# A hybrid attention step: queues ordered by a four-pass planner with due times, and one more query tile turned by VectorE and a transfer

## The chip, the cores and the metric

The kernel runs on one core of a Trainium2 chip. A core has a matrix engine (TensorE, PE in the profile; its weight loads are the row PEld), three engines for elementwise work (VectorE is DVE, ScalarE is ACT, GpSimd is POOL), a sync engine (SP) that in this kernel issues every transfer, and 16 DMA engines. Each engine works through its own queue in the order in which the program lists its instructions, and waits on semaphores. The metric is the device time of one execution, in microseconds, as the median of several runs.

## The reference, cut to what matters

One layer of a streaming encoder on 1024 prompt rows and 32 sample rows of width 1024, all in float32.

```python
qa, ka, va, ga, qb, kb, vb, gb = split(rmsnorm(h, g_pre) @ w_in)      # 1024 -> 8 x 512
# A: 8 heads of 64, band attention: a frame reads its own 64-frame chunk and the 8 before it
s = q @ k.T * ATTN_SCALE + bias_table[clip(k_pos - q_pos)];  oa = softmax(where(ok, s, NEG_INF)) @ v
# B: 8 heads of 64, stick-breaking attention, strictly causal
z = q @ k.T * ATTN_SCALE
log_1m = where(causal, log_sigmoid(-z), 0);  after = reverse_cumsum(log_1m) - log_1m
ob = where(causal, exp(log_sigmoid(z) + after), 0) @ v
y = concat(oa * silu(ga), ob * silu(gb)) @ w_out
h = h + rmsnorm(y, g_post)
h = h + sigmoid(h @ w_ple_gate) * (p @ w_ple)
```

The keys and values are returned too.

## The kernel before, in words

**Stages.** The rows are normalised, transposed and split into a high and a low half of fp32r (`hnh`, `hnl`), so that three fp32r matmuls make one float32 product. Then the 32 column blocks of `w_in` are multiplied (tiles `mm_qA`, `mm_kB`, ..., each in three chunks of 352 rows, 24 matmuls a chunk), woven with the attention of 16 heads, A and B in turn. The gates (`mm_gA`, `mm_gB`) come last and run beside the last head. Two Strassen-like stages follow: `w_out` (tiles `o0P` to `o3P`) and `w_ple_gate` (`g0P` to `g3P`).

**One head of B.** For each of eight query tiles `i` of 128 rows, `scores(i)` makes the scores against the `i + 1` key blocks up to it in PSUM (`SB`), ScalarE takes a Sigmoid into `om`, VectorE a running product (the scan), and GpSimd the difference of neighbours into `be`: the weights, query by key. TensorE needs them key by query. `weights_t(i)` turns them and splits the result into `wTh` (ScalarE's cast) and `wTl` (VectorE's subtraction). It has two ways:

- with TensorE: 128x128 transposes in groups of four into PSUM (`ptw`), from which the halves are made;
- for tiles named in `ROUND` (the dictionary `together`): VectorE turns 32x32 squares from `be` into `om`, a transfer writes `om` to a scratch tensor (`swap`), four transfers bring its quarters back into `be` in block order, and the halves are made from `be` in SBUF.

In `ROUND` before, tiles 4 and 6 of every head go the second way, of A and of B. Then `values(g)` multiplies the turned weights of four query tiles with the values (`PVB`). `attention_stream` lists the steps: tile `i`'s turning two units after its scores, and the values behind the last tile of a group of four. The last head of B runs from tile 7 down.

`om` and `be` are places in two rings of SBUF (`Arena`, 3076 and 3328 columns); a tile's place is given away when all its uses are done. The scores of tile 5 of B are 768 columns wide, those of tile 4 640, of tile 6 896.

**The order of the queues.** The program first only records its operations (`Recorder`). `Recorder.order` then lays them out on a model of the engines: at each step it takes the engine that can start first, and on it the waiting operation with the smallest key. The key is a class and the place in the program: class 0 for attention and 1 for projections on TensorE, `low` on the other engines. `cost` gives each operation's duration and how long after it its result can be used. A transfer is counted as an issue of 600 ns, 1500 ns of latency, the time of its bytes on one shared line, and 2000 ns of margin; a result that TensorE uses counts 400 ns more. The order that comes out is the order in which `emit` issues the instructions, so it is fixed when the program is built: on the chip, each engine waits in that order.

Of the kernel before, what the change touches and what calls it, by code (L numbers as in the profile page):

```python
# [8 lines left out]
F32 = mybir.dt.float32  # L9
F32R = mybir.dt.float32r  # L10
AF = mybir.ActivationFunctionType
# [16 lines left out]

ROUND = {"A": ((4,),(6,)), "B": ((4,),(6,))}
LAG_T = 2
LAG_V = 2
SPACE_S = 0.1
# [138 lines left out]


class Op:
    __slots__ = ("eng", "what", "args", "kw", "key", "busy", "late", "ready", "left", "after", "at", "size", "shared")


LAND = {"PE": 165, "ACT": 0, "DVE": 0, "POOL": 0, "SP": 0, "CTL": 0}
SEM = 60  # L180
MARGIN = 400
ISSUE = 600
DMA_NS, DMA_RATE, DMA_MARGIN = 1500, 320.0, 2000
DVE_SET, POOL_SET = 137, 110


# [77 lines left out]
class Recorder:  # L264
# [35 lines left out]
    def node(self, eng, what, args, kw, after):  # L300
        o = Op()
        o.eng, o.what, o.args, o.kw, o.after = eng, what, args, kw, after
        o.key = (self.cls if eng == "PE" else self.low, len(self.ops))
        o.shared = False
        self.ops.append(o)
        return o

    def add(self, eng, what, args, kw):
        writes, reads = [], []
        method = what[1] if isinstance(what, tuple) else ""  # L310
        for i, a in enumerate(args):
            if isinstance(a, (View, Raw, Segments)):
                (writes if i == 0 or (method == "tensor_tensor_reduce" and i == 7) else reads).append(a)
        for k, a in kw.items():
            if isinstance(a, (View, Raw, Segments)):
                (writes if k in ("out", "accum_out") else reads).append(a)
        o = self.node(eng, what, args, kw, set())
        for mine, write in ((reads, False), (writes, True)):
            for v in mine:
                b = v.buf  # L320
                hit = False
                for other, box, wrote in b.uses:
                    if other is not o and (write or wrote) and all(p < y and x < q for (p, q), (x, y) in zip(v.box, box)):
                        o.after.add(other)
                        hit = True
                if b.pool is not None:
                    if not hit:
                        o.after.add(b.place)
                    b.pool.ops.append(o)
                b.uses.append((o, v.box, write))  # L330
        o.busy, o.late = self.cost(eng, method, args, kw, writes, reads)
        o.shared = eng == "POOL"
        if eng == "DVE":
            sbuf = [v for v in reads if isinstance(v, (View, Segments)) and not v.buf.psum and v.free() > 4]
            o.shared = len(sbuf) > 1 or (method == "tensor_copy" and len(sbuf) == 1 and not writes[0].buf.psum)

    @staticmethod
    def cost(eng, method, args, kw, writes, reads):

        out = writes[0] if writes else None  # L340
        n = out.free() if isinstance(out, View) else 1
        psum = any(isinstance(v, (View, Segments)) and v.buf.psum for v in reads)
        if eng == "PE":
            if method == "transpose":
                return (109 if args[1].shape[0] > 64 else 62), 165
            return max(109.0, 2.5 + 0.449 * args[2].free()) * (1 if args[2].buf.dtype == F32R else 4), 165
        if eng == "ACT":
            return (60 if psum else 95) + 0.83 * n + (190 if "accum_out" in kw else 0), 105
        if eng == "DVE":
            if method == "tensor_tensor_scan":  # L350
                return 120 + 2.1 * n, 85
            if method == "tensor_copy" and not psum:
                return 70 + 0.53 * n, 85
            if method == "scalar_tensor_tensor":
                return 125 + 1.04 * n, 85
            if method == "tensor_tensor_reduce":
                return 90 + 1.04 * n, 150
            return 70 + 1.04 * n, 85
        if eng == "POOL":
            if method == "tensor_tensor":  # L360
                if n == 1:
                    return 535, 40
                return 170 + (1.77 if out.buf.dtype == F32 else 2.15) * n, 40
            if method == "tensor_scalar":
                return 255 + 0.86 * n, 0
            return 100 + 0.82 * n, 0
        size, run = 4, 0
        for v in (out, args[1]):
            if isinstance(v, View) and v.buf.pool is not None:
                size, run = 4 * v.shape[0] * v.free(), 4 * v.shape[-1]  # L370
        return ISSUE, max(size / DMA_RATE, size / run * (8.5 + 0.0365 * run) / 16)


    def order(self):

        import heapq
        for place, old in self.turns:
            place.after.update(x[0] for x in old.uses)
        users = {id(o): [] for o in self.ops}
        for o in self.ops:  # L380
            o.left, o.ready = len(o.after), 0.0
            for a in o.after:
                users[id(a)].append(o)
        names = ("PE", "ACT", "DVE", "POOL", "SP", "CTL")
        free = dict.fromkeys(names, 0.0)
        soon = {e: [] for e in names}
        now = {e: [] for e in names}
        for o in self.ops:
            if not o.left:
                heapq.heappush(soon[o.eng], (0.0, o.key, id(o), o))  # L390
        out, port, line = [], 0.0, 0.0
        while len(out) < len(self.ops):
            best = None
            for e in names:
                if now[e]:
                    t = free[e]
                elif soon[e]:
                    t = max(free[e], soon[e][0][0])
                else:
                    continue  # L400
                if best is None or t < best[0]:
                    best = (t, e)
            t, e = best
            while soon[e] and soon[e][0][0] <= t:
                _, key, n, o = heapq.heappop(soon[e])
                heapq.heappush(now[e], (key, n, o))
            o = heapq.heappop(now[e])[2]
            if o.shared and e == "DVE" and port > t + DVE_SET:
                held = [x for x in now[e] if not x[2].shared]
                if held:  # L410
                    heapq.heappush(now[e], (o.key, id(o), o))
                    pick = min(held)
                    now[e].remove(pick)
                    heapq.heapify(now[e])
                    o = pick[2]
            o.at = t
            if e == "CTL":
                done = t
            elif e == "SP":
                free[e] = t + o.busy  # L420
                line = max(line, t + o.busy + DMA_NS) + o.late
                done = line + DMA_MARGIN
            else:
                if o.shared:
                    t = max(t, port - (DVE_SET if e == "DVE" else POOL_SET))
                    port = t + o.busy
                free[e] = t + o.busy
                done = t + o.busy + o.late
            out.append(o)
            for u in users[id(o)]:  # L430
                if u.eng == e and e != "SP":
                    r = t if e == "CTL" else free[e] if e == "PE" else done
                else:
                    r = done + (0 if u.eng == "CTL" else SEM + (MARGIN if u.eng == "PE" else 0))
                u.ready = max(u.ready, r)
                u.left -= 1
                if not u.left:
                    heapq.heappush(soon[u.eng], (u.ready, u.key, id(u), u))
        return out


    def emit(self, tc):
# [15 lines left out]
def stream_step(  # L458
# [79 lines left out]
    def load_w(j):  # L538

        if j >= len(order) or j in raws:  # L540
            return
        kind, p = order[j]
        c0 = NAMES.index(kind) * 512 + p * P
        raws[j] = []
        for kh in range(2):
            raw = wpool.tile([P, 4, P], F32, tag="wr", name=f"wr_{kind}{p}_{kh}", bufs=4)
            dma(raw, w_in[0, kh * 512:(kh + 1) * 512, c0:c0 + P].rearrange("(k p) c -> p k c", p=P))
            raws[j].append(raw)
# [243 lines left out]
    def attention(ab, p, h):  # L792
# [16 lines left out]

        together = {i: g for g in ROUND[ab] for i in g}  # L810
        whole, done_with = {}, []
# [901 lines left out]
    for m, (nm, src, group) in enumerate(sets):  # L1713
        last_set = m == len(sets) - 1
        state = [{}, {}]
        for n, prod in enumerate(ORDER):
            for pair, t in enumerate(group):
# [43 lines left out]
                if nm == "o":  # L1761
# [4 lines left out]
                    if prod == "P6":  # L1766
                        add(up, st["p1"], bank, ALU.add)
# [101 lines left out]
```

## Time and profile before

| | before |
|---|---|
| median of 3 runs | 804.93 us (804.59 to 805.31) |
| the profiled execution | 809.23 us |
| its span, first to last instruction | 807.4 us |
| granted TensorE clock, mean | 0.998 |
| TensorE busy | 788.0 us, 98% of the span |
| VectorE, ScalarE, GpSimd busy | 70%, 62%, 54% |
| moved by the DMA engines | 161.09 MB, 199 GB/s on average |

A busy time is the time in which at least one instruction of the engine is under way. Matmuls overlap, so their mean durations add up to more than the busy time. All operations are issued from one line of the program (`emit`, L452), so the rows are told apart by the tiles they write and read (out<-in).

### The profile page before, as it was taken

What the parts mean: (1) busy time and instruction counts of PE and PEld (TensorE: products, weight loads), DVE (VectorE), ACT (ScalarE), POOL (GpSimd) and SP (SyncE); (2) the same over time, 40 slices, a digit from 0 to 9 for tenths busy, and PEclk for the clock granted to TensorE, in tenths of its full rate; (3) what the DMA queues carried; (4) which work ended last, traced back from release to release, by engine and by line L of the source; (5) the groups of instructions that cost most, each with busy time, mean ns of one, the idle gap of its engine ahead of it and who ended that gap; (6) DMA issues with size and microseconds to landing.
All of it is one profiled execution on the core that took longest, in us unless ns stands there. A gap on an engine that the chain in (4) does not pass through costs nothing.

```text
span 807.4 us, 14271 instructions
## 1 busy us (share of the span) xinstructions
PE 788.0 (98%) x4646; PEld 722.3 (89%) x4646; DVE 567.9 (70%) x1007; ACT 504.4 (62%) x1061; POOL 432.1 (54%) x503
## 2 busy tenths in 40 slices
PE   8999989999999999999999999999999999999997
PEld 7899989899989999899999989999997777878786
DVE  7626768786588788788886688765435787477655
ACT  5636774676586646795675696543327977877641
POOL 5623655764356668134551236777542549598513
PEclk9999999999999999999999999999999999999999
DMA  8419895667878749854535667765569948869633
GB/s 276 149 45 293 215 253 175 195 185 217 225 225 246 215 121 267 216 146 133 151 81 169 147 175 212 234 199 152 166 207 322 298 147 270 278 218 302 215 108 131
DMA packets 160973, 161.09 MB, mean 199 GB/s; under 512 B 39154, under 2 KB 120794, under 8 KB 160899
## 3 DMA queue, kind: packets, MB, share of 16 engines
q1 hardware_dynamic: 160898, 160.18, 67.1%
q8 instruction: 37, 0.61, 0.3%
q14 instruction: 38, 0.30, 0.1%
HBM read 99.23 MB, written 52.49 MB: 188 GB/s over the span
## 4 chain that ended last, share of the span: by engine, by line
PE 72%; DMA 6%; ACT 6%; POOL 5%; DVE 5%; issue 4%; SPq 2%; DVEq 0%; POOLq 0%; ACTq 0%
PE mm_gA L452 6%; PE mm_gB L452 6%; PE mm_kA L452 5%; PE mm_qA L452 5%; PE mm_qB L452 4%; PE SB L452 3%; PE mm_vA L452 3%; PE PVB L452 3%; PE mm_kB L452 3%; PE PVA L452 3%; PE mm_vB L452 3%; PE SA L452 2%; PE o1P L452 2%; PE g2P L452 2%; PE g3P L452 2%
## 5 line engine op out<-in xcount | busy, mean ns | idle before, releaser
L452 POOL TENSOR_TENSOR be<-om 128x128 f32<-128x128 f32 (+7 forms) x64 | 75.4, 1184 | 64.8 <-DVE om L452 29.0
L452 DVE TENSOR_TENSOR_SCAN om<-om,SB 128x384 f32<-128x384 f32 (+5 forms) x96 | 94.9, 1001 | 9.1 <-ACT om L452 7.4
L452 ACT ACTIVATE om<-SB 128x384 f32<-128x384 f32 (+5 forms) x96 | 44.4, 493 | 36.0 <-DVE SB L452 26.9
L452 ACT ACTIVATE be<-om,statA 128x640 f32<-128x640 f32 (+3 forms) x64 | 44.4, 694 | 18.2 <-DVE statA L452 11.0
L452 DVE TENSOR_TENSOR wTl<-be,wTh 128x640 fp32r<-128x640 f32 (+1 forms) x32 | 37.6, 1175 | 10.3 <-ACT wTh L452 8.8
L452 ACT CAST wTh<-ptwB 128x512 fp32r<-128x512 f32 (+3 forms) x64 | 29.5, 481 | 19.6 <-PE ptwB L452 15.4
L452 DVE TENSOR_TENSOR wTl<-ptwB,wTh 128x512 fp32r<-128x512 f32 (+3 forms) x64 | 33.7, 545 | 10.3 <-ACT wTh L452 7.8
L452 DVE TENSOR_TENSOR wTl<-ptwA,wTh 128x512 fp32r<-128x512 f32 (+2 forms) x64 | 29.8, 483 | 15.7 <-ACT wTh L452 12.5
L452 POOL TENSOR_TENSOR oB<-oB,oB 128x256 f32<-128x256 f32 x32 | 27.7, 882 | 18.6 <-DMA oB<-in_w_out_dram 10.5
L452 DVE STREAM_TRANSPOSE om<-be 128x640 f32<-128x640 f32 (+1 forms) x32 | 28.9, 904 | 9.8 <-POOL be L452 4.9
L452 PE MATMUL SB<-kdB,LB 128*128 128x384 f32 (+5 forms) x96 | 34.0, 357 | 1.6 <-DVE om L452 1.6
L452 DVE CUSTOM_DVE_ANT_0 om<-SA,biasA 128x320 f32<-128x320 f32 (+3 forms) x64 | 29.5, 482 | 7.6 <-PE SA L452 4.4
L452 ACT CAST wTh<-ptwA 128x512 fp32r<-128x512 f32 (+2 forms) x64 | 26.2, 426 | 13.3 <-PE ptwA L452 7.5
L452 PE MATMUL SB<-klB,LB 128*128 128x384 f32 (+5 forms) x96 | 32.9, 345 | 0.0
L452 PE MATMUL SA<-kdA,LA 128*128 128x320 f32 (+2 forms) x96 | 30.2, 325 | 0.7 <-DVE LA L452 0.4
L452 POOL TENSOR_TENSOR sggA<-sggA,oggA 128x352 f32<-128x352 f32 x24 | 23.8, 991 | 11.2 <-DVE sggA L452 10.8
L452 PE MATMUL SA<-klA,LA 128*128 128x320 f32 (+2 forms) x96 | 29.6, 320 | 0.0
L452 ACT CAST wTh<-be 128x640 fp32r<-128x640 f32 (+1 forms) x32 | 25.0, 782 | 6.4 <-DMA swapA<-om 3.3
L452 PE MATMUL ptwB<-ident,be 128*128 128x128 f32 x192 | 28.7, 273 | 0.0
L452 PE MATMUL ptwA<-ident,be 128*128 128x128 f32 x160 | 26.3, 276 | 2.0 <-ACT be L452 1.8
L452 DVE TENSOR_TENSOR SB<-SB,maskb 128x128 f32<-128x128 f32 x64 | 17.3, 287 | 13.5 <-PE SB L452 13.1
L452 POOL TENSOR_TENSOR klA<-stkA,kdA 64x1024 fp32r<-64x1024 f32 x8 | 20.7, 2587 | 8.2 <-ACT kdA L452 7.7
(707 smaller groups left out, 2650.5 us busy)
## 6 DMA issues: line engine op xcount, KB each, us to landing
swapA<-om SPq DMA_DIRECT2D x16, 320.0 KB, 2.8
be<-swapA SPq DMA_DIRECT2D x64, 80.0 KB, 3.9
oB<-in_w_out_dram SPq DMA_DIRECT2D x16, 256.0 KB, 4.9
sum_dro<-oB SPq DMA_DIRECT2D x16, 256.0 KB, 3.3
gB<-in_w_ple_gate_dram SPq DMA_DIRECT2D x16, 256.0 KB, 4.6
sum_drg<-gB SPq DMA_DIRECT2D x16, 256.0 KB, 3.8
x<-in_x_prompt_dram SPq DMA_DIRECT2D x16, 256.0 KB, 5.2
h_dr<-h SPq DMA_DIRECT2D x8, 512.0 KB, 3.3
```

Of the source, the lines that this page charges most:

```text
L452: getattr(getattr(tc.nc, o.what[0]), o.what[1])(*args, **kw)
```

## The change

It has two parts.

1. `ROUND` for B names tile 5 as well, as a group of its own: `((4,),(5,),(6,))`. In each of the 8 heads of B this tile goes the second way: one transpose of squares on VectorE, one transfer out and four back, and the halves from SBUF, in place of six TensorE transposes and two pairs of halves from PSUM.
2. `order` makes four plans instead of one. After each of the first three, `due` goes through the plan from its end and gives every operation of ScalarE, VectorE, GpSimd and SP a new key: the latest time at which it can start so that its users start on time, where a TensorE operation's time is the one that it had in that plan. TensorE's own keys stay. The fourth plan is used. The costs are changed as well: 30 ns more for operations of ScalarE and VectorE and for GpSimd's `tensor_tensor`, a start-up delay for each engine that waits (`WAKE`), 1310 ns when ScalarE changes between Exp and Sigmoid, and for a transfer 520 ns of issue, the time of its bytes, and 2500 ns until it has landed, plus 200 ns for the engine that waits for it.

```diff
-ROUND = {"A": ((4,),(6,)), "B": ((4,),(6,))}
+ROUND = {"A": ((4,),(6,)), "B": ((4,),(5,),(6,))}
...
 SEM = 60
-MARGIN = 400
-ISSUE = 600
-DMA_NS, DMA_RATE, DMA_MARGIN = 1500, 320.0, 2000
+WAKE = {"PE": 400, "ACT": 100, "DVE": 100, "POOL": 190, "SP": 0}
+ISSUE = 520
+DMA_RATE, LANDING, WAKE_DMA = 320.0, 2500, 200
+TABLE_NS = 1310
...
+            o.table = next((a for a in args if a in (AF.Exp, AF.Sigmoid)), None) if eng == "ACT" else None
...
-            return (60 if psum else 95) + 0.83 * n + (190 if "accum_out" in kw else 0), 105
+            return (90 if psum else 125) + 0.83 * n + (190 if "accum_out" in kw else 0), 105
...
     def order(self):
...
+        best, end = self.plan(users)
+        for _ in range(3):
+            self.due(best, users, end)
+            out, last = self.plan(users)
+            if last >= end and 0:
+                break
+            best, end = out, last
+        return best
+
+    def due(self, out, users, end):
+        late, after = {}, {}
+        for o in reversed(out):
+            e = o.eng
+            t = after.get(e, end) if 0 and e != "CTL" else end
+            for u in users[id(o)]:
+                v = late[id(u)]
+                if u.eng == e and e not in ("SP", "CTL"):
+                    v -= 0.0 if e == "PE" else o.late
+                elif u.eng != "CTL":
+                    v -= SEM + WAKE[u.eng] + (WAKE_DMA if e == "SP" and u.eng != "SP" else 0) + o.late * (e != "SP")
+                elif e != "SP":
+                    v -= o.late
+                if e == "SP":
+                    v -= LANDING + o.late
+                t = min(t, v)
+            if e == "PE":
+                late[id(o)] = o.at
+                continue
+            late[id(o)] = t - o.busy if e != "CTL" else t
+            if e != "CTL":
+                after[e] = late[id(o)]
+                o.key = (late[id(o)], o.key[1])
+
+    def plan(self, users):
...
             elif e == "SP":
                 free[e] = t + o.busy
-                line = max(line, t + o.busy + DMA_NS) + o.late
-                done = line + DMA_MARGIN
+                line = max(line, free[e]) + o.late
+                done = line + LANDING
             else:
+                if o.table and o.table != table:
+                    table = o.table
+                    t = max(free[e] + TABLE_NS, t)
...
-                    r = done + (0 if u.eng == "CTL" else SEM + (MARGIN if u.eng == "PE" else 0))
+                    r = done + (0 if u.eng == "CTL" else SEM + WAKE[u.eng] + (WAKE_DMA if e == "SP" and u.eng != "SP" else 0))
...
-        return out
+        return out, max(free.values())
```

More of the change, by code (lines that the diff above doesn't have):

```diff
@@ L175 @@
 class Op:
-    __slots__ = ("eng", "what", "args", "kw", "key", "busy", "late", "ready", "left", "after", "at", "size", "shared")
+    __slots__ = ("eng", "what", "args", "kw", "key", "busy", "late", "ready", "left", "after", "at", "size", "shared", "table")
 LAND = {"PE": 165, "ACT": 0, "DVE": 0, "POOL": 0, "SP": 0, "CTL": 0}
 SEM = 60
-MARGIN = 400
-ISSUE = 600
-DMA_NS, DMA_RATE, DMA_MARGIN = 1500, 320.0, 2000
+WAKE = {"PE": 400, "ACT": 100, "DVE": 100, "POOL": 190, "SP": 0}
+ISSUE = 520
+DMA_RATE, LANDING, WAKE_DMA = 320.0, 2500, 200
+TABLE_NS = 1310
 DVE_SET, POOL_SET = 137, 110
@@ L303, in node @@
         o.key = (self.cls if eng == "PE" else self.low, len(self.ops))
-        o.shared = False
+        o.shared, o.table, o.busy, o.late = False, None, 0.0, 0.0
         self.ops.append(o)
@@ L347, in cost @@
         if eng == "ACT":
-            return (60 if psum else 95) + 0.83 * n + (190 if "accum_out" in kw else 0), 105
+            return (90 if psum else 125) + 0.83 * n + (190 if "accum_out" in kw else 0), 105
         if eng == "DVE":
             if method == "tensor_tensor_scan":
-                return 120 + 2.1 * n, 85
+                return 150 + 2.1 * n, 85
             if method == "tensor_copy" and not psum:
-                return 70 + 0.53 * n, 85
+                return 100 + 0.53 * n, 85
             if method == "scalar_tensor_tensor":
-                return 125 + 1.04 * n, 85
+                return 155 + 1.04 * n, 85
             if method == "tensor_tensor_reduce":
-                return 90 + 1.04 * n, 150
-            return 70 + 1.04 * n, 85
+                return 120 + 1.04 * n, 150
+            return 100 + 1.04 * n, 85
         if eng == "POOL":
@@ L361, in cost @@
                 if n == 1:
-                    return 535, 40
-                return 170 + (1.77 if out.buf.dtype == F32 else 2.15) * n, 40
+                    return 565, 40
+                return 200 + (1.77 if out.buf.dtype == F32 else 2.15) * n, 40
             if method == "tensor_scalar":
@@ L374, in order @@
     def order(self):
-        import heapq
         for place, old in self.turns:
@@ L380, in order @@
         for o in self.ops:
-            o.left, o.ready = len(o.after), 0.0
             for a in o.after:
                 users[id(a)].append(o)
+        best, end = self.plan(users)
[30 more added lines that the diff above has]
+    def plan(self, users):
+        import heapq
+        for o in self.ops:
+            o.left, o.ready = len(o.after), 0.0
         names = ("PE", "ACT", "DVE", "POOL", "SP", "CTL")
@@ L390, in order @@
                 heapq.heappush(soon[o.eng], (0.0, o.key, id(o), o))
-        out, port, line = [], 0.0, 0.0
+        out, port, line, table = [], 0.0, 0.0, None
         while len(out) < len(self.ops):
```

## The prediction

> **What bounds the kernel now.** I read the page's busy times first, then busy time by stage, then TensorE's waits, the chain, and last the rows of the work that the change moves. The page's busy times:
>
> ```profile
> span 807.4 us, 14271 instructions
> ...
> PE 788.0 (98%) x4646; PEld 722.3 (89%) x4646; DVE 567.9 (70%) x1007; ACT 504.4 (62%) x1061; POOL 432.1 (54%) x503
> ```
>
> By stage (the stretch, each engine's busy time, the clock granted to TensorE, the DMA engines' share and rate):
>
> ```profile
> core 0: us, PE busy (x) PEld busy (x) DVE busy (x) ACT busy (x) POOL busy (x), PEclk, DMA share, GB/s
> 0.00:31.00 31.00, 26.64 (x143) 23.01 (x144) 19.13 (x28) 17.12 (x33) 21.41 (x40) 1.00 0.82 268
> ...
> 60.00:110.00 50.00, 46.85 (x295) 45.24 (x294) 31.86 (x75) 34.69 (x76) 24.34 (x27) 0.97 0.93 256
> 110.00:300.00 190.00, 186.34 (x1193) 178.08 (x1193) 150.73 (x264) 119.39 (x260) 113.52 (x147) 1.00 0.71 203
> 300.00:500.00 200.00, 197.49 (x1266) 188.70 (x1265) 158.31 (x305) 138.87 (x296) 88.66 (x100) 1.00 0.61 167
> 500.00:610.00 110.00, 110.00 (x695) 107.81 (x694) 62.33 (x101) 46.86 (x100) 68.14 (x72) 1.00 0.66 197
> ...
> 803.00:808.00 5.00, 0.00 (x0) 0.00 (x0) 1.54 (x4) 0.39 (x1) 0.44 (x1) 0.94 0.30 105
> ```
>
> TensorE works 788.0 of 807.4 us; every other engine is idle 30% or more. Its 19.4 us of idleness lie in few places: 4.4 at the start (31.00 less 26.64), 5.0 after its last matmul, and 3.15 + 3.66 + 2.51 = 9.3 us in the attention stages from 60 to 500 us. From 500 to 610 it has none. So the time is a sum of TensorE's work; the change can take work off it, or change these idle stretches. What ended them (in all, times, longest):
>
> ```profile
> PE PVA L452 <- ACT wTh L452: 2.7, 1, 2.7
> ...
> PE ptwA L452 <- ACT be L452: 1.8, 2, 1.3
> PE SB L452 <- DVE om L452: 1.6, 3, 0.9
> ...
> PE ptkA L452 <- DVE wTl L452: 1.3, 1, 1.3
> ```
>
> The largest, read in the timeline of ACT and PE and in the busy time of two short stretches:
>
> ```profile
> 100.19 0.41 SPq L452 DMA_DIRECT2D swapA<-om  x1
> ...
> 103.31 0.72 ACT L452 CAST wTh<-be 128x640 fp32r<-128x640 f32 x1 [3.30 <-DMA swapA<-om]
> 104.08 1.29 PE L452 MATMUL PVA<-wTh,v2A 128*128 128x512 f32 x4 [2.73 <-ACT wTh L452]
> ```
>
> ```profile
> 101.35:104.10 2.75, 0.02 (x2) 0.02 (x1) 0.04 (x1) 0.80 (x2) 1.31 (x2) 1.00 0.95 284
> 104.10:108.00 3.90, 3.90 (x14) 3.70 (x15) 3.07 (x4) 3.90 (x9) 1.74 (x5) 0.56 1.05 245
> ```
>
> ACT stands 3.30 us at the cast of a turned tile (wTh<-be), which waits for a transfer; TensorE runs dry for 2.75 us, and the granted clock is then 0.56 for 3.90 us, which loses another 3.90 x 0.44 = 1.7 us. One late swap costs 4.46 us. This is the price list of the change: it adds such swaps and reorders everything around them. [...]
>
> **Part 1: tile 5 of B leaves TensorE.** Each of B's 8 heads turned tile 5 (six 128x128 blocks) by six TensorE transposes in two groups, of 4 and 2; 8 x 6 = 48 of the 192 in the first row below go.
>
> ```profile
> L452 PE MATMUL ptwB<-ident,be 128*128 128x128 f32 x192 | 28.7, 273 | 0.0
> ...
> L452 ACT CAST wTh<-ptwB 128x512 fp32r<-128x512 f32 x32 | 18.4, 587 | 16.5 <-PE ptwB L452 12.7 <-PE PVB L452 3.5
> ...
> L452 ACT CAST wTh<-ptwB 128x256 fp32r<-128x256 f32 x16 | 6.0, 376 | 1.0 <-PE ptwB L452 0.9
> ...
> L452 ACT CAST wTh<-be 128x640 fp32r<-128x640 f32 x24 | 17.4, 726 | 4.9 <-DMA swapA<-om 3.3 <-DMA be<-swapA 1.3 <-PE PVB L452 0.2
> ...
> L452 ACT CAST wTh<-be 128x896 fp32r<-128x896 f32 x8 | 7.6, 948 | 1.5 <-DMA be<-swapB 1.5
> ...
> L452 DVE TENSOR_TENSOR wTl<-ptwB,wTh 128x512 fp32r<-128x512 f32 x32 | 21.4, 680 | 8.6 <-ACT wTh L452 6.2 <-PE PVB L452 2.4
> ...
> L452 DVE TENSOR_TENSOR wTl<-ptwB,wTh 128x256 fp32r<-128x256 f32 x16 | 6.6, 413 | 0.5 <-ACT wTh L452 0.4
> ...
> L452 DVE TENSOR_TENSOR wTl<-be,wTh 128x640 fp32r<-128x640 f32 x24 | 26.3, 1097 | 6.6 <-ACT wTh L452 6.3
> ...
> L452 DVE TENSOR_TENSOR wTl<-be,wTh 128x896 fp32r<-128x896 f32 x8 | 11.3, 1410 | 3.7 <-ACT wTh L452 2.4 <-DMA out_dram<-vtA 0.9
> ...
> L452 DVE STREAM_TRANSPOSE om<-be 128x640 f32<-128x640 f32 x24 | 20.1, 836 | 7.7 <-ACT be L452 4.4 <-POOL be L452 3.2
> ...
> L452 DVE STREAM_TRANSPOSE om<-be 128x896 f32<-128x896 f32 x8 | 8.9, 1107 | 2.2 <-POOL be L452 1.7 <-POOL om L452 0.4
> ```
>
> One group of four in the timeline:
>
> ```profile
> 258.97 0.60 PE L452 MATMUL ptwB<-ident,be 128*128 128x128 f32 x4
> ```
>
> TensorE: four transposes take 0.60 us together and one alone 0.273, so each after the first adds (0.60 - 0.273) / 3 = 0.11 us. In a full stream 48 x 0.11 = 5.3 us go; the busy row's share, 28.7 x 48 / 192 = 7.2, counts tails that lie over other matmuls and is the upper end. I take 5.3, all on the path.
>
> VectorE: it gains one square transpose of 768 columns, midway between 836 and 1107: 0.97 us, and one subtraction of 768 from SBUF, midway between 1097 and 1410: 1.25; it loses the two subtractions from PSUM, 0.68 + 0.41. Net 1.13 us a head, 9.1 us in all. Cover: its idle time of 39 us in 110:300 and 42 us in 300:500; without it, 9.1 us would be paid. ACT: one cast of 768 (midway between 726 and 948: 0.84) for 0.59 + 0.38, so 1.0 us less in all. Nothing of it is on the path as long as the order fits.
>
> Transfers: per head one store of 128 x 768 x 4 B = 384 KB, and four quarters of 96 KB back. What such transfers take, from the rows of DMA issues (KB each, median us to landing):
>
> ```profile
> swapB<-om SPq DMA_DIRECT2D x8, 448.0 KB, 4.2
> be<-swapB SPq DMA_DIRECT2D x32, 112.0 KB, 2.9
> ...
> swapB<-om SPq DMA_DIRECT2D x8, 320.0 KB, 2.3
> ...
> be<-swapB SPq DMA_DIRECT2D x32, 80.0 KB, 3.6
> ```
>
> What their issue takes on SP's queue (ns, least, median and most), and the end of B's attention in the chain:
>
> ```profile
> L452 SPq DMA_DIRECT2D be<-swapB x64: 303/430/2376, 132.7 to 571.9; - x64
> ```
>
> ```profile
> 585.66 1.21 PE PVB L452 x8
> 587.33 21.50 PE mm_gB L452 x133
> ```
>
> Out 2.3 to 4.2 us, back 2.9 to 3.6, three issues of 0.43 between: some 6.5 to 9 us from issue to last landing. The queue of SP gets 40 more issues (8 x 5 x 0.43 = 17 us in all); behind a store that waits for the squares, and quarters that wait for the store, stand the loads of weights, caches and gates on the same queue. On ACT the new cast waits for the last quarter; behind it stand the Sigmoids and the copies that empty TensorE's banks, for which TensorE waits in turn. The cover: tile 5 is used only by V1, which the stream puts two units later, behind tiles 6 (swapped already) and 7. The arenas' places of tile 5 are held for these microseconds longer, as those of tiles 4 and 6 are now. In the last head, which runs from tile 7 down, the chain shows 21.5 us of gate matmuls (133 of them) behind the last PVB: time enough. So the part costs nothing beyond, if ACT doesn't reach the cast early.
>
> **Part 2: the planner.** The order of all queues is now that of a fourth plan, in which jobs of ACT, VectorE, POOL and SP go by the latest start that the plan before leaves them; TensorE keeps its ranks. The costs change too: 30 ns more for each ACT and VectorE job, 1.31 us for a change of ACT's table, wake-ups by engine, and less for transfers. No row shows the new order. Bounds: at best all 9.3 us of idleness between 60 and 500 and the 1.7 us of slow clock go, -11.0; at worst new stalls of 4.46 each, which I bound at three, +13.4. I take half of the idleness, -4.6: two of the four waits above, 1.8 us behind an ACT job and 1.3 behind a VectorE one, are of the sort that ranking by need moves forward; the late swap is not, since the plan now allows transfers less. The idle start, the end and the last stages I leave as they are.
>
> Sum: 809.23 us for the profiled execution (span 807.4 and 1.8 around) - 5.3 - 4.6 = 799.3. The runs' median is 804.93, 4.30 below that execution; less the same 9.9 us it comes to 795.0.
>
> **The rivals.**
>
> *Transposes only.* The new order trades waits for equal ones: 804.93 - 5.3 = 799.6. For it: the idleness is spread over many short waits, which follow from the plan's error and not from its ranks.
>
> *All the idleness goes.* -5.3 - 9.3 - 1.7 = -16.3: 788.6. For it: the plan knows costs that it didn't know (the table loads). Against: two passes or four, it still sees no contention.
>
> *Late swaps, slower.* The plan counted a 96 KB quarter as ready for ACT 0.60 + 1.50 + 0.31 + 2.00 + 0.06 = 4.47 us after its issue, and now 0.52 + 0.31 + 2.50 + 0.36 = 3.69, of which 3.33 is the landing; the rows have 3.6 and 2.9 for B's quarters, so some land later than planned, and the number of B's round trips rises from 16 to 24. Each that is late by enough halts ACT at a cast, as at 103.31. It decides from two such stalls on (2 x 4.46 = 8.9 against 5.3); three give -5.3 + 13.4 = +8.1: 813.0. Against: of 24 casts of 640 columns the trace shows only 4.9 us of ACT's waiting, 3.3 of it that one case; and a late cast hurts only when TensorE has nothing else at its head.
>
> *One more such stall:* -5.3 + 4.46 = -0.8, 804.1, within 0.2% (1.6 us), about what a measurement of this kernel can tell from no change.
>
> *VectorE sets the pace.* Its 9.1 us come on the path: +9.1 - 5.3 = +3.8, 808.7. Against: it is idle 39 of 190 us where B's heads run. [...]
>
> That the change does not do what it says: the tuple (5,) reaches the same branch as (4,) and (6,), so it will; but the fourth plan is taken even where the third was shorter, which is a reason for the slower rival.
>
> **How the numbers follow.** Chances: forecast 0.37, transposes only 0.15, all the idleness 0.10 (faster 0.62); one more stall 0.07 (same); late swaps 0.27 and VectorE 0.04 (slower 0.31). The predicted time is the likeliest, 795.0. The range runs from 785.0 (the best case, 788.6, with the 7.2 in place of 5.3 for the transposes and some 2 us of the start) to 813.0 (three late swaps). The cases that are faster alone span 788 to 800.
>
> **What would show it.** Right: 144 transposes ptwB in place of 192, eight rows' worth of STREAM_TRANSPOSE and CAST wTh<-be at 128x768, VectorE near 577 us, TensorE's busy time near 782, and its idleness in the attention stages under 6 us. Wrong: idleness there of 12 us or more with ACT's waits for swapB or swapA at their ends, PEclk under 1.00 in more than one stage (late swaps); DVE over 90% in a stage with TensorE waiting for wTl (VectorE); or TensorE idle in 610:803, where this forecast moves nothing.

## The result: 5 us faster, and the profile after

The changed kernel takes 799.19 us (median of 9 runs, 796.71 to 803.30) against 804.44 for the kernel before (9 runs beside it, 802.38 to 805.31). The ratio is 0.9938, 95% interval 0.9919 to 0.9956: faster by 0.6%. The forecast was 795.0 in a range of 785 to 813. The sign is right, the size is half of what was forecast. The profiled execution took 802.72 us and its span is 800.7, 6.7 us below the one before. Both profiles are of executions above their medians, 809.23 before and 802.72 after, so what is read from them holds for one execution each. The page's busy times, and then the same stages as before:

```profile
span 800.7 us, 14262 instructions
...
PE 780.7 (98%) x4598; PEld 716.9 (90%) x4598; DVE 580.3 (72%) x1007; ACT 501.2 (63%) x1051; POOL 442.2 (55%) x503
```

```profile
0.00:31.00 31.00, 29.14 (x155) 24.93 (x156) 20.86 (x33) 20.16 (x38) 21.37 (x41) 1.00 0.85 263
...
60.00:110.00 50.00, 47.42 (x309) 45.71 (x307) 37.17 (x82) 34.89 (x76) 23.84 (x27) 1.00 0.97 269
110.00:300.00 190.00, 184.60 (x1172) 176.24 (x1172) 151.56 (x257) 117.00 (x255) 120.53 (x153) 1.00 0.74 215
300.00:500.00 200.00, 196.42 (x1258) 188.94 (x1258) 165.40 (x313) 139.71 (x299) 92.28 (x100) 1.00 0.69 189
500.00:610.00 110.00, 110.00 (x682) 106.69 (x681) 62.28 (x100) 48.63 (x99) 68.44 (x70) 1.00 0.69 211
```

TensorE's busy time falls by 7.3 us, from 788.0. Of this, 1.7 is the stretch of half clock after 104 us, which the second table no longer has (60:110 shows 1.00 where it was 0.97). How much of the rest is the 48 transposes' can't be read here: the new planner alone (below), which keeps all of them, is at 784.1. Its idle time is 20.0 us where it was 19.4. At the start it is 1.9 instead of 4.4. From 60 to 500 us it is 2.58 + 5.40 + 3.58 = 11.6 instead of 9.3: the half of that idleness that was forecast to go did not go, more came. The rows of the moved work:

```profile
L494 PE MATMUL ptwB<-ident,be 128*128 128x128 f32 x144 | 22.2, 274 | 0.5 <-POOL be L494 0.5
...
L494 DVE STREAM_TRANSPOSE om<-be 128x768 f32<-128x768 f32 x8 | 7.8, 970 | 2.4 <-POOL be L494 1.7 <-POOL om L494 0.5
...
L494 DVE TENSOR_TENSOR wTl<-be,wTh 128x768 fp32r<-128x768 f32 x8 | 8.4, 1048 | 3.2 <-ACT wTh L494 3.2
...
L494 ACT CAST wTh<-be 128x768 fp32r<-128x768 f32 x8 | 6.7, 834 | 7.5 <-DMA be<-swapB 7.1 <-PE PVB L494 0.4
```

Everything that was to move has moved, at about the durations that were worked out; the subtraction is faster, 1.05 us for 1.25. ACT waits 7.5 us before the new casts, and 19.3 before all casts of swapped tiles (below) where it was 6.4. TensorE's own waits (in all, times, longest), and its longest one in the timeline:

```profile
PE ptwA L494 <- ACT sumrowA L494: 2.7, 1, 2.7
PE SB L494 <- DVE om L494: 1.9, 1, 1.9
...
PE mm_kB L494 <- ACT stkB L494: 1.2, 1, 1.2
```

```profile
106.87 0.47 SPq L494 DMA_DIRECT2D o_dr<-otA  x1
...
107.38 4.01 SPq L494 DMA_DIRECT2D be<-swapA  x8
...
110.56 0.25 ACT L494 COPY sumrowA<-ptsA 8x128 f32<-8x128 f32 x1 [3.69 <-DMA o_dr<-otA]
...
110.87 0.66 PE L494 MATMUL ptwA<-ident,be 128*128 128x128 f32 x4 [2.75 <-ACT sumrowA L494]
```

The late swap at 104 us is gone, and another wait on a transfer stands in its place: ACT's copy needs a buffer of the tag `ot` whose store was issued at 106.87 and has not landed when the copy's turn comes; ACT stands 3.69 us, TensorE 2.75.

### The profile page after: what moved, and what is told of

Its sections match the earlier page's. It is cut to its first block, busy times and chain, and to the rows that moved or that the text cites. A ratio compares the mean times of both kernels' runs of the same rounds, so it can differ in the third digit from the quotient of the medians.

```text
span 800.7 us, 14262 instructions
## 1 busy us (share of the span) xinstructions
PE 780.7 (98%) x4598; PEld 716.9 (90%) x4598; DVE 580.3 (72%) x1007; ACT 501.2 (63%) x1051; POOL 442.2 (55%) x503
## 4 chain that ended last, share of the span: by engine, by line
PE 66%; DMA 10%; DVE 4%; SPq 3%; ACT 3%; POOL 2%; issue 2%; DVEq 0%; ACTq 0%; POOLq 0%
PE mm_gB L494 6%; PE mm_gA L494 6%; PE mm_vB L494 4%; PE SB L494 3%; PE mm_kA L494 3%; PE mm_qB L494 3%; PE PVA L494 3%; SPq L494 3%; PE mm_qA L494 3%; PE PVB L494 3%; PE mm_kB L494 3%; PE g0P L494 2%; PE o0P L494 2%; PE g1P L494 2%; PE o1P L494 2%; PE mm_vA L494 2%
## 5 line engine op out<-in xcount | busy, mean ns | idle before, releaser
L494 POOL TENSOR_TENSOR be<-om 128x896 f32<-128x896 f32 (+7 forms) x64 | 78.6, 1234 | 75.5 <-DVE om L494 29.8
L494 DVE TENSOR_TENSOR wTl<-be,wTh 128x640 fp32r<-128x640 f32 (+2 forms) x40 | 46.2, 1160 | 15.5 <-ACT wTh L494 15.3
L494 ACT ACTIVATE be<-om,statA 128x640 f32<-128x640 f32 (+4 forms) x64 | 44.5, 696 | 9.9 <-PE ptwA L494 4.0
L494 ACT CAST wTh<-be 128x640 fp32r<-128x640 f32 (+2 forms) x40 | 31.7, 792 | 19.3 <-DMA be<-swapB 11.3
L494 DVE STREAM_TRANSPOSE om<-be 128x640 f32<-128x640 f32 (+2 forms) x40 | 36.5, 913 | 4.5 <-POOL be L494 3.6
L494 ACT CAST wTh<-ptwB 128x512 fp32r<-128x512 f32 (+3 forms) x48 | 21.9, 483 | 13.7 <-PE ptwB L494 13.2
L494 DVE TENSOR_TENSOR wTl<-ptwB,wTh 128x512 fp32r<-128x512 f32 (+3 forms) x48 | 25.2, 543 | 3.6 <-ACT wTh L494 2.5
L494 POOL TENSOR_TENSOR klB<-stkB,kdB 64x1024 fp32r<-64x1024 f32 x8 | 19.5, 2438 | 13.0 <-ACT kdB L494 9.3
L494 POOL TENSOR_TENSOR gB<-gB,gB 128x256 f32<-128x256 f32 x32 | 24.8, 796 | 3.5 <-DMA gB<-in_w_ple_gate_dram 3.3
```

Source lines behind the costliest of these rows:

```text
L494: getattr(getattr(tc.nc, o.what[0]), o.what[1])(*args, **kw)
```

## The experiments

All ratios are against the kernel before in runs beside it, with 95% intervals. They differ by up to 0.1% from the quotients of the medians; microseconds of a change are worked out from the ratios.

### The two parts apart, and the price of 48 transposes

Tile 5 alone, in the kernel before: `ROUND["B"] = ((4,),(5,),(6,))`.

> The old planner and its costs; only the tuple (5,) is added for B. Theory 1 (the gain is the 48 transposes off TensorE and nothing else, the planner's ranks give nothing): 5.3 us less than before, 799.1, ratio 0.993. Theory 2 (the turn by squares pays only in an order that expects it, so the gain is the planner's): no gain, 802 to 808, with new waits of ACT for swapB. Theory 3 (every re-planning reshuffles the order, and the luck of the order is some 3 us either way, as large as the gain): anything from 796 to 803.

Measured 812.95, ratio 1.0083 (1.0063 to 1.0103): slower by 0.8%.

The planner alone, in the changed kernel: `ROUND["B"] = ((4,),(6,))`.

> The new planner, ranks and costs; tile 5 of B stays with TensorE's transposes. Theory 1: 804, the same as before within 0.2%; its idleness at the start falls by 2.5 us as after the whole change, and that in the attention stages rises by about 2. Theory 2: about 799, ratio 0.994, the whole gain. Theory 3: anything from 800 to 808.

Measured 799.31, ratio 0.9914 (0.9895 to 0.9933): the whole gain, and not told apart from the whole change.

The kernel before in its own order, with tile 5's transposes issued twice:

```diff
                     getattr(getattr(tc.nc, o.what[0]), o.what[1])(*args, **kw)
+                    if o.what[1] == "transpose" and o.args[0].buf.name.startswith("ptwB") and "_5_" in o.args[0].buf.name:
+                        getattr(getattr(tc.nc, o.what[0]), o.what[1])(*args, **kw)
```

> The kernel before in its own order, unchanged, with each of the 48 transposes of tile 5 of B issued twice, so that the price of 48 transposes is measured without any re-planning. All theories: 48 x 0.11 = 5.3 us more, 809.8, ratio 1.0066. If the transposes cost their share of busy time, 7.2 us: 811.7. If the order hides them in waits, less than 3 us.

Measured 812.05, ratio 1.0071 (1.0047 to 1.0095): 0.71% of 805.51 is 5.7 us (3.8 to 7.7), near the 5.3 of the forecast, though 7.2 is not excluded. So the price is borne out, and added transposes do lie on the path. Yet turning the tile by squares in their place gives nothing: not with the old planner (it costs 0.8%, 6.7 us), and not with the new (0.9914 without, 0.9938 with). Theory 1 falls. Theory 3 expected 796 to 803 and 800 to 808, and both runs lie outside. Theory 2, that the gain is the planner's, holds, for the planner with the constants that it has here (below). The planner alone by stages:

```profile
60.00:110.00 50.00, 47.20 (x308) 45.49 (x306) 34.20 (x82) 34.61 (x76) 23.99 (x30) 1.00 0.96 264
110.00:300.00 190.00, 186.89 (x1188) 180.80 (x1189) 149.12 (x261) 120.20 (x261) 119.27 (x152) 0.98 0.73 206
300.00:500.00 200.00, 199.95 (x1293) 193.41 (x1292) 161.51 (x310) 141.38 (x305) 90.20 (x99) 1.00 0.63 173
```

TensorE's idleness from 60 to 500 is 2.80 + 3.11 + 0.05 = 6.0 us, and in 300:500 there is next to none. The whole change has 11.6, and 3.58 in 300:500. The difference of 5.6 us is about the price of the transposes, but two profiles of one execution each don't show that it is the same 5.6. The 0.98 is a stretch of 6.8 us at half clock (PEclk 0.50, last section), from 111.2 us on, which costs the planner alone 3.4 us and which the whole change doesn't have.

### Ranks or costs

One plan in place of four, all else as changed: `for _ in range(0)`.

> The whole change but for the repeated planning: the first plan is used, with the new costs and the old keys (place in the program), and tile 5 turned by squares. Theory 1: as after the change, 799, since the ranks give nothing. If the ranks by due time do work, it is slower than the whole change by what they give, 3 us or more: 802 and over. If the ranks harm, it is faster: 796 or less.

Four plans with the old costs:

```diff
-WAKE = {"PE": 400, "ACT": 100, "DVE": 100, "POOL": 190, "SP": 0}
-ISSUE = 520
-DMA_RATE, LANDING, WAKE_DMA = 320.0, 2500, 200
-TABLE_NS = 1310
+WAKE = {"PE": 400, "ACT": 0, "DVE": 0, "POOL": 0, "SP": 0}
+ISSUE = 600
+DMA_NS, DMA_RATE, LANDING, WAKE_DMA = 1500, 320.0, 2000, 0
+TABLE_NS = 0
...
```

> The whole change with the old costs: four plans and ranks by due time, tile 5 turned by squares, but durations, issue, landing, margins and no table loads as before. With the old ranks it took 813 under the old costs and 807 under the new; the new ranks under the new costs take 799. If ranks and costs add up: 813 - 7.5 = 805.5. If the ranks work only with the new costs, since a due time is as good as the costs that it is reckoned from: 810 or more. If the ranks alone do it: 799 to 801.

All four with tile 5 turned by squares:

| | ranks by place in the program | ranks by due time |
|---|---|---|
| old costs | 1.0083 (1.0063 to 1.0103) | 0.9974 (0.9961 to 0.9987) |
| new costs | 1.0011 (0.9991 to 1.0032) | 0.9938 (0.9919 to 0.9956) |

One plan took 806.67 us, as expected if the ranks work (802 and over); the old costs took 802.58, between "the ranks alone" (799 to 801) and "ranks and costs add up" (805.5). In these four orders the ranks are worth 1.1% under the old costs and 0.7% under the new, the costs 0.7% and 0.4%. So the ranks appear as the larger part and work without the new costs; but each cell of the table is a single order, and the last section of experiments shows what another order can be worth.

### Where the transposes' gain went

Theory L: late quarters, at which ACT stands. Theory V: the work added on VectorE, 9.1 us net by the forecast's estimate. Two runs take the late quarters away and leave that work in place. In the first, tile 5's halves are made from the squares, without transfers:

```diff
+                here = w1
+                if (ab, i) == ("B", 5):
+                    here = w0[:, 0:m * P]
+                else:
+                    dr = scratch([P, m * P], f"swap{nm}_{i}")
...
-                turned = w1.rearrange("p (g b q) -> p g b q", g=4, q=32)
+                turned = here.rearrange("p (g b q) -> p g b q", g=4, q=32)
```

> The whole change, but tile 5 of B is not sent out and back: its squares are turned by VectorE, and the halves are made at once from them (the blocks are not exchanged, so that part of the work is left out). VectorE's and ACT's work is as in the whole change; 8 stores, 32 quarters and their waits are gone. Theory L (the transposes' 5.3 us are eaten because the plan allows a landing 2.5 us, and ACT then stands at the cast of a late quarter): the idleness of TensorE from 60 to 500 us falls from 11.6 to about 6, as in the planner alone, and the time is 5 us below the whole change, 794. [...]

In the second the plan allows transfers more: `LANDING = 3500`.

> The whole change with LANDING 3500 in place of 2500, so that the plan counts a quarter of 96 KB as landed 4.3 us after its issue; the whole change's trace has a median of 4.1. Theory L: ACT's waits for swapB and swapA before its casts fall from 17.9 us to under 9, and the time from 799 to 795. Theory V: 799. Theory O (the luck of the order): 796 to 803, without a tie to ACT's waits.

Measured: without transfers 800.42, ratio 0.9937 (0.9912 to 0.9961), the same as the whole change; TensorE idles 10.6 us from 60 to 500, where theory L expected about 6. But VectorE's work was not as in the whole change: the subtraction of this tile, read from the squares, took 12.9 us in all in place of 8.4, and VectorE was busy 585.7 us in place of 580.3.

```profile
L494 DVE TENSOR_TENSOR wTl<-om,wTh 128x768 fp32r<-128x768 f32 x8 | 12.9, 1611 | 2.3 <-ACT wTh L494 2.2
```

With the longer allowance 809.02, ratio 1.0041 (1.0024 to 1.0058): slower, though ACT's waits for transfers before the casts fell from 17.9 to 10.3 us, not quite under the 9 expected. First the whole change, then this run:

```profile
L494 ACT CAST wTh<-be 128x640 fp32r<-128x640 f32 (+2 forms) x40 | 31.7, 792 | 19.3 <-DMA be<-swapB 11.3 <-DMA be<-swapA 6.6 <-PE PVB L494 1.3
```

```profile
L494 ACT CAST wTh<-be 128x640 fp32r<-128x640 f32 (+2 forms) x40 | 31.8, 794 | 10.7 <-DMA be<-swapB 5.2 <-DMA be<-swapA 5.1
```

Neither run bears theory L out: in the first tile 5's transfers are gone and the time stays, in the second ACT's waits are nearly halved and the time rises. Neither is a clean test, since each has an order of its own and the first has more work on VectorE. Theory V, VectorE's added work, and theory P, that the attention stages are paced by a tile's chain through the other engines, were put to two more runs. Tile 5 not turned at all (as the run without transfers, with `here = w1` and the squares left out too):

> The whole change, but tile 5 of B is not turned at all: no TensorE transposes, no squares, no transfers; the halves are made from the unturned weights (that part of the work is left out). Theory V (VectorE's added work, 9.1 us net, eats the 5.3 us): the squares, 7.8 us of VectorE, are gone, so the 5.3 us come out: 794, and TensorE's idleness from 60 to 500 us is near the planner alone's 6.0. Theory P (the attention stages are paced by the chain of one tile through POOL, VectorE, ACT and the rings, and less work on TensorE there only turns into idleness): about 799, idleness 10 to 12. Theory O (the luck of the order, which the 20 ns more of landing put at 2 us): 796 to 803.

The planner alone, with work added to VectorE only:

```diff
+            if (ab, i) == ("B", 5):
+                nc.vector.tensor_tensor(w1, w1, w1, ALU.max)
             for b in range(0, n, 4):
```

> The planner alone, with tile 5 of B still on TensorE's transposes, and one VectorE instruction more on each of the 8 tiles of 768 columns, ahead of its transposes: the larger of the weights and themselves, which changes no value, about 0.95 us each, 7.6 us in all, with two operands from SBUF. TensorE's work is that of the planner alone. Theory V: 4 to 6 us more than the planner alone's 799, 803 to 805, with more idleness of TensorE in 60 to 500. Theory P: 1 to 3 us more. If VectorE's idle time hides it: 799.

Measured: not turned 806.72, ratio 1.0036 (1.0017 to 1.0055); VectorE's work added 801.22, ratio 0.9959 (0.9941 to 0.9977), 0.45% or 3.6 us above the planner alone by the ratios (about 1.5 to 5.7 from the two intervals). The added work was more than expected: 1.34 us a tile and 10.8 in all, not 7.6. And in the run that turns nothing VectorE was not relieved: the squares' 7.8 us are gone, but its subtractions took longer (the 768 columns 1381 ns, in the whole change 1048), and it was busy 581.5 us, in the whole change 580.3.

```profile
L494 DVE TENSOR_TENSOR be<-be 128x768 f32<-128x768 f32 x8 | 10.8, 1344 | 0.1
```

```profile
L494 DVE TENSOR_TENSOR wTl<-be,wTh 128x768 fp32r<-128x768 f32 x8 | 11.1, 1381 | 1.7 <-ACT wTh L494 1.7
```

Busy time in 110:300 and 300:500, first of the run that turns nothing, then of the one with VectorE's work added:

```profile
110.00:300.00 190.00, 184.25 (x1148) 176.15 (x1149) 151.00 (x251) 121.47 (x256) 116.98 (x148) 0.98 0.69 201
300.00:500.00 200.00, 195.81 (x1251) 188.40 (x1250) 162.81 (x308) 137.25 (x297) 92.90 (x103) 0.99 0.64 168
```

```profile
110.00:300.00 190.00, 187.69 (x1202) 180.12 (x1203) 163.11 (x269) 122.02 (x265) 121.40 (x151) 1.00 0.71 206
300.00:500.00 200.00, 198.98 (x1286) 192.03 (x1285) 160.53 (x310) 138.14 (x300) 91.45 (x102) 1.00 0.63 172
```

With nothing put in place of the transposes, TensorE still idles 2.55 + 5.75 + 4.19 = 12.5 us from 60 to 500. With the transposes kept and VectorE busier than in the whole change (587.3 us against 580.3), it idles 6.4 in the profiled execution. That speaks against V, as far as idleness goes. The times decide nothing: 3.6 us lie between what V (4 to 6) and P (1 to 3) expected for 7.6 us of work, and the run that turns nothing doesn't test V, since VectorE is as busy in it as in the whole change. The same sum (50, 190 and 200 us less busy) over all profiles, each of one execution:

| tile 5 of B | idle 60 to 500 us, of it 300 to 500 |
|---|---|
| TensorE: before; transposes doubled | 9.3, 2.5; 8.6, 2.9 |
| TensorE: planner alone; VectorE's work added | 6.0, 0.05; 6.4, 1.0 |
| TensorE: planner alone, LANDING 2000; 3500 (below) | 8.4, 1.2; 8.9, 1.3 |
| off TensorE: old planner; one plan; due ranks with old costs | 14.0, 6.5; 16.4, 4.8; 9.3, 5.0 |
| off TensorE: whole change; LANDING 2520 (below); 3500 | 11.6, 3.6; 11.8, 4.9; 11.0, 3.1 |
| off TensorE: no transfers; not turned | 10.6, 3.4; 12.5, 4.2 |

From 60 to 500 TensorE idles 6.0 to 9.3 us wherever it turns the tile, and 9.3 to 16.4 wherever it doesn't; in 300:500 it is 0.05 to 2.9 against 3.1 to 6.5. In 300:500 the gap between the two sets is narrow, but no profile of one lies within the other. Two of the profiles are far from typical: before, 4.8 us above its median, and one plan, the slowest of 12 executions and 7.0 above the median. Idleness where work was taken off is what P expects. But V is not excluded, since VectorE is busy 580 to 589 us in all eight profiles without the transposes and 568 to 572 in five of the six with them; only the run with VectorE's work added parts the two.

P's time for the run that turns nothing, 799, was missed (806.7). Its profile has three stretches of 3.4 us at half clock ahead of the end, 5.1 us lost, and the whole change's has none. In the medians this is about half: the granted clock is 0.992 on average over its 12 runs and 0.997 over the whole change's 9, which is 6.3 against 2.2 us, some 4 of the 7.5 between the medians.

Which link of the chain paces the stages, and how much of the 5.3 us VectorE's added work alone would explain, stays open. So does whether the transposes' price would come out in a fixed order: doubling them kept the order, but no run leaves them out of an order that stays as it is, and every run without them has new places for all operations.

### How much is the luck of the order

The whole change with LANDING 2520 in place of 2500; the planner alone with 3500 and with 2000:

> The whole change with LANDING 2520 in place of 2500, a change that means nothing but makes the plan anew: it measures the luck of the order. Theory O: 3 us or more away from the whole change's 799, either way. Theories L and V: within 1.5 us of it.

> The new planner alone (tile 5 of B on TensorE), with LANDING 3500. Theory L: it has fewer late quarters to cure, ACT waited 7.9 us for them: 797 to 798, against 799 of the planner alone. Theory V: 799. Theory O: 796 to 803.

> The planner alone with LANDING 2000 in place of 2500. With 3500 it took 816, with 2500 799. If a shorter allowance for transfers is what the order gains from: 796 or less, below both kernels. If 2500 is about what transfers take here and less lets ACT stand at casts: 801 to 805, ACT's waits for quarters over 8 us. Theory O: 796 to 803 without a tie to either.

| | LANDING 2000 | 2500 | 2520 | 3500 |
|---|---|---|---|---|
| whole change | | 0.9938 | 0.9964 (0.9941 to 0.9987) | 1.0041 |
| planner alone | 1.0001 (0.9986 to 1.0015) | 0.9914 | | 1.0131 (1.0098 to 1.0164) |

20 ns moved the whole change by 0.26%, 2.1 us, which the two intervals don't tell from none: less than theory O's 3 and more than the 1.5 of L and V. The planner alone with 3500 took 816.12, outside all that was expected. With 2000 it took 804.57 and ACT waited 10.5 us for quarters, as expected if 2500 is about what transfers take here; but it waited only 8.8 with 3500, against 8.1, so those waits don't follow the time. The planner alone is 0.9% slower with less allowance, all that it had gained, and 2.2% slower with more. The run with 3500 loses much of its time in a stage that has no swaps at all; its longest waits, of which the first and the third lie there, and the stage:

```profile
PE o0P L494 <- ACT oB L494: 3.8, 1, 3.8
PE ptwA L494 <- ACT sumrowA L494: 3.1, 1, 3.1
PE o2P L494 <- DVE h L494: 2.1, 1, 2.1
```

```profile
610.00:790.00 180.00, 174.15 (x785) 137.62 (x784) 125.43 (x194) 129.16 (x263) 103.13 (x99) 0.99 0.71 233
```

5.85 us of idleness there, where the planner alone has 0.69. The profile also loses 6.8 us to half clock, where the planner alone loses 3.4. One constant of the plan reorders all 800 us. Whether 2500 is a good order by luck or near a best value, three points don't tell.

No run beat the whole change beyond the intervals. The planner alone has the lowest ratio, 0.9914, and needs less of SP's queue and of the transfers.

## Why the prediction was right, and where its sum was wrong

Sign and range held, the sign by one of the two terms only, and in a range of 28 us, which holds the time before as well. The likeliest case did not: it was off by 4.2 us. The rival *transposes only* named 799.6, next to the 799.2 measured, by luck: its reason is wrong, since tile 5 alone made the kernel slower.

- **The 48 transposes, -5.3 us.** The price was borne out: 5.7 (3.8 to 7.7) measured by doubling them in a fixed order. The step that failed is "all on the path", read as if what costs when added pays when removed: with the new planner, taking them off TensorE gave nothing (0.9914 with them, 0.9938 without). In all eight profiles without them TensorE idles more in 300:500 than in any of the six with them. Why the work comes back as idleness stays open.
- **The squares' cover.** The prices of VectorE (0.97 and 1.25 us; measured 0.97 and 1.05) and of ACT held, though VectorE's busy time rose by 12.4 us and not 9.1. The part was said to cost nothing beyond; with the old planner it cost 0.8% in all.
- **The planner, -4.6 us.** Alone it gave 0.86%, 6.9 us of 804.9. The step's size was low and its place right in part: between the two profiles idleness in 60 to 500 us fell from 9.3 to 6.0, and at the start (0:31) from 4.4 to 2.4, which the forecast had left as it was. The half was taken of 9.3, with the late swap's 2.75 in it, and subtracted from a median that lay 4.30 below the profiled execution, about that swap's 4.46. The doubled run, in the same order, has no such stall (0.5 us idle in 60:110), so most executions may not have it; only one of them has a profile. That the plan sees no contention, as the rival *all the idleness goes* had it, is not so: in both kernels it keeps operations of VectorE and GpSimd apart that it marks as `shared`.
- **The sum.** The two terms were added. They don't add: +0.8% and -0.9% apart, -0.6% together. The 5.0 us read as idle behind the last matmul are 4.4, since the row runs past the span's end; the sum doesn't use them.
- **Late swaps.** ACT's waits before these casts did rise, from 6.4 to 19.3 us, as that rival said. No run shows that they decided: without tile 5's transfers the time is the same. Its price of 4.46 us for a stall is not general: the whole change has a wait of 2.75 us with no half clock behind it.
- **VectorE sets the pace.** 10.8 us of added work cost 3.6 us (about 1.5 to 5.7): more than the forecast's nothing, less than this rival's whole. That run has a new order too, so the cost is not VectorE's alone for certain.
- **Signs named ahead.** 144 transposes, VectorE near 577 (580.3), TensorE near 782 (780.7) were met; idleness under 6 us was not. At 11.6 it came close to the 12 that was named as a sign of being wrong.

## What to carry to other kernels

TensorE, 98% busy here, had a price for added work (5.7 us for 48 transposes), and taking the same 48 off it, under the new planner, gave nothing back (0.9914 with them, 0.9938 without). So double the work first, then leave it out altogether, in the same order, and only then pay for a replacement. A change that rebuilds the whole order needs a control that rebuilds it for no reason, since here one constant of the plan moved the time by up to 2% (799.31 us to 816.12). A control that leaves work out has to be read for what else it changed: the two here changed VectorE's time in a way that wasn't meant (subtractions of 1611 and 1381 ns in place of 1048). Two parts of a change are worth a run each before their terms are added.

## What the runs showed of the hardware

The granted clock of TensorE was halved after some of its gaps and not after others: for 3.4 us after one of 2.02 us and for 6.8 us after one of 3.6, and not at all after one of 2.75. In the run that turns nothing a gap of 2.02 us ended at 149.11, and this is the clock around it:

```profile
143.00:148.50 5.50, 4.08 (x27) 3.69 (x25) 5.50 (x4) 4.74 (x9) 5.50 (x8) 1.00 0.67 138
149.00:152.40 3.40, 3.29 (x12) 3.29 (x13) 3.40 (x6) 1.62 (x3) 0.00 (x0) 0.50 0.69 192
```

In the planner alone, a wait of 3.6 us was followed by 6.8 us at half clock:

```profile
111.20:118.00 6.80, 5.97 (x22) 5.97 (x23) 3.71 (x7) 4.82 (x10) 3.02 (x6) 0.50 0.82 231
```

In the whole change a gap of 2.75 us that ended at 110.87 left the clock at 1.00 (110:300 in its table shows no loss). In the profile before, a gap of the same 2.75 us that ended at 104.08 was followed by a granted clock of 0.56 for 3.90 us. So in these four cases the length of the gap alone does not tell whether the clock halves, and no run shows what else decides. The 3.40 us at a clock of 0.50 cost 1.7 us on top of the gap, the 6.80 us 3.4.
